# Gathering tokens feature-major for two experts at a time in a mixture-of-experts layer

## The chip, the cores and the metric

The kernel runs on one core of one Trainium2 chip. The metric is the device time of the whole kernel in microseconds; the median of the runs shown counts.

## What is computed

One layer on 256 tokens of width 2048, all in float32: an attention and state-space mixer, a layer norm, then sixteen experts of which each token uses two, and a per-layer embedding (PLE) that is gated by the same tokens. The change concerns the experts:

```python
combine = jnp.einsum('tk,tke->te', top_w, jax.nn.one_hot(top_idx, N_EXPERTS, dtype=f32))
out = jnp.zeros((b * s, d), f32)
for e in range(N_EXPERTS):
    hid = jax.nn.silu(xt @ w_gate[e]) * (xt @ w_up[e])
    out = out + combine[:, e:e + 1] * (hid @ w_down[e])
...
gate = jax.nn.sigmoid(jnp.einsum('bsd,de->bse', x, w_ple_gate))
return gate * jnp.einsum('bsk,kd->bsd', p_i, w_ple)
```

Here xt is the normed x, w_gate and w_up are 2048 x 1024 for each expert, and w_down is 1024 x 2048. The layer's last step is `layer_norm(DEEPNORM_ALPHA * h + moe + ple, ln2_g, ln2_b)`.

## The kernel before

The mixer, the first norm and the router take the first 447 us; the change does not touch them but for names of buffers. Then come the experts, one after the other, and a final norm from about 1480 us.

Each expert has places for CAP = 64 tokens. The one-hot matrix oh (128 tokens of a half x 64 places, doubled to 128 columns) says which token sits in which place. `gather(e)` multiplies it with h, the normed tokens before gain and bias: oh is stationary (64 columns), h moves in pieces of 512 columns (L679). That yields rows (places x features), which ACT copies to SBUF (L681) and which eight transposes (L689) turn to features x places; two DVE operations each (L693, L694) apply the norm's gain and bias and leave xg. Two transposes of oh (L697) give cm, the map that later returns the rows to the tokens, and two matmuls (L699) with the token weights cw give cwp, the weight of each place.

`gate_up(e)` takes 16 weight tiles of 1 MiB (128 x 2048 float32), eight of the gate and eight of the up matrix, and multiplies with xg stationary (L715). `hidden` makes the sigmoid (ACT L723), two products (DVE L724, L725, the second also by cwp), four transposes (L728) and ACT's copy hidT (L730). `down(e)` takes 8 tiles (L762, L784 in the last expert), and splits the result y into a high and a low part (ACT L752, DVE L753). `give_back` multiplies both with cm (L739), in the PSUM banks py, and DVE adds them to acc (L743). The banks py are also those that y comes from. Other PSUM banks are mt (gathers, transposes), gu (gate, up) and pl (PLE).

Weights run through a ring of sixteen tiles. SP issues each load once its slot is free (L76, L82, L87, L95 are its four buffers' lines), with at most eight loads under way. The order of loads is that of use: for each expert gate and up alternating, then down; ahead of experts 1, 4, 8 and 12 come four tiles of the PLE gate and one of ple, used behind the expert's down (`ple_gate`, L805 and L819). The order on each engine is made by a scheduler when the kernel is built; it pushes PLE matmuls and the next expert's gate matmuls between steps of the give-back.

After expert OV_AT = 6's hidden, `overflow` stands: all engines read a flag (how many tokens found no place) and branch past a loop over all experts (L826 reads it, L834 branches). With these inputs the loop is skipped, but SP, ACT and the others join there, and the buffers that the loop would use (tags y, xg, w2) are tied to it. The gather of expert e + 1 is written between hidden and down of expert e.

Of the kernel before, what the change touches and what calls it, by code (L numbers as in the profile page):

```python
# [27 lines left out]
OV_AT = 6  # L28
# [504 lines left out]
def back(ctx, tc, i, out, fr, dbg=lambda *a: None):  # L533
# [74 lines left out]
    r4 = mp.tile([128, 256], F32, name="r4", tag="cm", bufs=2)  # L608
# [58 lines left out]
    def gather(e):  # L667


        oh = mp.tile([128, NT, 2, CAP], F32, name="oh", tag="oh")  # L670
        for t in range(NT):
            nc.vector.tensor_scalar(oh[:, t], i1[:, None, :].to_broadcast([128, 2, CAP]), pos[:, t, e:e + 1], None,
                                    op0=OP.is_equal)
        rows = mp.tile([128, 1024], F32, name="rows", tag="y")
        for c in range(2):
# [6 lines left out]
        xg = mp.tile([128, 8, 2, CAP], F32, name="xg", tag="xg")  # L682
        b = [128, 4, 2, CAP]
        for c in range(2):
            ps = mt_psum(b)
            js = slice(4 * c, 4 * c + 4)
            for j in range(4):
                col0 = c * 512 + j // 2 * 256
                nc.tensor.transpose(ps[:, j].rearrange("p a b -> p (a b)"),  # L689
                                    rows[:, col0 + j % 2:col0 + 256:2], ident)  # L690
            gain, bias = (lnT[:, n, :].rearrange("p (d j) -> p j d", d=2)[:, js, :, None].to_broadcast(b)
                          for n in range(2))
            nc.vector.tensor_tensor(xg[:, js], ps, gain, op=OP.mult)  # L693
            nc.vector.tensor_tensor(xg[:, js], xg[:, js], bias, op=OP.add)  # L694
        ps = mt_psum([128, 512])
        for t in range(NT):
            nc.tensor.transpose(ps[:, t * 128:(t + 1) * 128], oh[:, t].rearrange("p a b -> p (a b)"), ident)  # L697
        for t in range(NT):
            nc.tensor.matmul(ps[:, 256:257], oh[:, t].rearrange("p a b -> p (a b)"), cw[:, t, e:e + 1],  # L699
                             start=t == 0, stop=t == 1)  # L700
        cm = mp.tile([128, 256], F32R, name="cm", tag="cm", bufs=2)
        cwp = mp.tile([128, 1], F32, name="cwp", tag="cwp", bufs=2)
        nc.scalar.activation(cm, ps[:, :256], AF.Copy)
        nc.vector.tensor_copy(cwp, ps[:, 256:257])
        return xg, cm, cwp

    def gate_up(e, xg):
        pgu = [psum.tile([128, 512], F32, name="pgu", tag="gu", bufs=2) for _ in range(2)]
        for k2 in range(8):
            for j in range(2):  # L710
                w = v2(ring.take(("gu"[j], e, k2)), FE)
                for r in range(2):
                    k = 2 * k2 + r
                    for fh, hs in H2:
                        mm = nc.tensor.matmul(pgu[j][hs], xg[:, k % 8, k // 8, :], w[:, r, fh * 512:(fh + 1) * 512],  # L715
                                         start=k == 0, stop=k == KB - 1)
            ring.fill()
        return pgu, mm

    def hidden(pgu, cwp):  # L720

        hid = mp.tile([128, 512], F32, name="hid", tag="w2", bufs=3)
# [10 lines left out]
    def give_back(cm, y, cols, n, pss):  # L733

        for t in range(NT):
            ps = pss(t)
            for j in range(2):
                for dh, hs in H2:
                    nc.tensor.matmul(ps[dh], cm[hs, t * 128:(t + 1) * 128], y[cols // 512][j][hs, cols % 512:cols % 512 + n],  # L739
                                     start=j == 0, stop=j == 1)  # L740
            for dh, hs in H2:
                a = acc[:, t, dh * 1024 + cols:dh * 1024 + cols + n]
                nc.vector.tensor_tensor(a, a, ps[dh], op=OP.add)  # L743

    def y_parts():
        y0 = mp.tile([128, 2, 512], F32R, name="y0", tag="y")
        y1 = [mp.tile([128, 512], F32R, name="y1", tag="w2", bufs=3) for _ in range(2)]
        return (y0[:, 0, :], y0[:, 1, :]), y1
# [6 lines left out]
    def down(e, hidT, cm):  # L755
# [13 lines left out]
        for c in range(2):  # L769
            def pss(t):  # L770
                p2 = psum.tile([128, 2, 512], F32, name="py", tag="y", bufs=1)
                return p2[:, 0, :], p2[:, 1, :]
            give_back(cm, y, c * 512, 512, pss)

    def down_last(e, hidT, cm):
        py = psum.tile([128, 2, 512], F32, name="py", tag="y", bufs=1)
        y = y_parts()
        for q in range(4):
# [11 lines left out]
            give_back(cm, y, q * 256, 256, pss)  # L790
# [18 lines left out]
    def ple_gate(c):  # L809
# [4 lines left out]
        for t in range(NT):  # L814
            sg = mp.tile([128, 512], F32, name="sg", tag="w2", bufs=3)
# [8 lines left out]
    def overflow():  # L824
# [9 lines left out]
        with tc.If(n_over > 0):  # L834
            with tc.For_i(0, NE, 1) as e:
                ovc = mp.tile([128, NT], F32, name="ovc")
                nc.sync.dma_start(ovc, scro[bass.ds(e, 1)].rearrange("o t p -> p (o t)"))
                oT = [mp.tile([128, 4, 256], F32, name="oT", tag=tag) for tag in ("y", "xg")]
                hd, *ow = [mp.tile([128, 512], F32, name="ow", tag="w2", bufs=3) for _ in range(3)]
                for fh in range(2):  # L840
# [8 lines left out]
                    for t in range(NT):  # L849
# [6 lines left out]
                        nc.scalar.activation(oT[fh][:, :, t * 128:(t + 1) * 128], ps, AF.Copy)  # L856
                for c in range(4):
                    cs = slice(c * 512, (c + 1) * 512)
                    pys = psum.tile([128, 2, 512], F32, name="py", tag="y", bufs=1)
                    for f in range(8):  # L860
                        w = wload(ow[f % 2], i["w_down"], e, f * 128, c * 512)
                        fh, j = divmod(f, 4)
                        for t in range(NT):
                            nc.tensor.matmul(pys[:, t, :], oT[fh][:, j, t * 128:(t + 1) * 128], w,
                                             start=f == 0, stop=f == 7)
# [7 lines left out]
    xg, cm, cwp = gather(0)  # L873

    lna = const.tile([16, 2, 128], F32, name="lna")
    with tc.issue_after(stats_done.ins):
        nc.vector.tensor_scalar(lna, fr.lnr[:, 0:2, :], ALPHA, None, op0=OP.mult)
# [23 lines left out]
    for e in range(NE):  # L901
        pgu, gated = gate_up(e, xg)
        hidT, cm_e = hidden(pgu, cwp), cm
# [5 lines left out]
        if e + 1 < NE:  # L909
            xg, cm, cwp = gather(e + 1)  # L910
            down(e, hidT, cm_e)
        else:
            down_last(e, hidT, cm_e)
        if e == 0:
# [14 lines left out]
            ovT = const.tile([NE, NT, 128], F32, name="ovT")  # L929
# [55 lines left out]
```

## Time and profile before

| | |
|---|---|
| Median of three runs | 1504.21 us (1503.3 to 1505.61) |
| The profiled execution | 1501.48 us, span 1499.8 us |
| Mean granted TensorE clock | 0.987 |
| TensorE busy | 1422.9 us, 95% of the span |
| DVE, ACT, POOL busy | 477.0, 291.9, 63.4 us |
| Moved | 499.96 MB, mean 333 GB/s |

The span runs from the first to the last instruction. TensorE's busy time is the sum of its matmuls; weight loads overlap it and are counted apart. The mean load rate hides that the rate differs from stretch to stretch.

### The profile page before, as it was taken

Reading aid. Unit: us, or ns where it says so; the run is one execution under the profiler, and the core shown is the slowest. Engines: PE = TensorE matmul, PEld = TensorE weight load, DVE = VectorE, ACT = ScalarE, POOL = GpSimd, SP = SyncE. Lnnn points to the kernel's source line nnn. Section 1 sums busy time; section 2 is a strip of 40 time slices with the busy share of each in tenths; the row PEclk is TensorE's granted clock in tenths of the full one; section 3 lists DMA queues with packets and bytes.
Section 4 is the critical chain, followed back from the end, with each engine's and each line's share of the span. In section 5 each row is a group of like instructions: output and inputs, shape, how many; then the busy total and the mean of one; then the engine's idle time right before and its main releaser. Section 6 shows DMA issues by size and latency. Waiting matters only on the chain. (4 is left out here: it accounts for less than half of the span.)

```text
span 1499.8 us, 15718 instructions
## 1 busy us (share of the span) xinstructions
PE 1422.9 (95%) x6467; PEld 703.5 (47%) x6467; DVE 477.0 (32%) x825; ACT 291.9 (19%) x445; POOL 63.4 (4%) x80
## 2 busy tenths in 40 slices
PE   7999999999989999999999989999999999999994
PEld 5878878777863433333233323323333332343332
DVE  4476774545651222112012211201221220202126
ACT  3465554444330010001010000000000000110001
POOL 3000011200000000000000000000000000000002
PEclk9999999999999999999999989999999999999997
DMA  8655555467858699999989999999999999899993
GB/s 275 186 171 167 190 192 194 155 224 291 291 188 341 264 420 392 417 420 410 352 332 420 419 419 377 409 420 369 420 419 420 420 409 412 365 420 420 420 386 118
DMA packets 116721, 499.96 MB, mean 333 GB/s; under 512 B 12692, under 2 KB 25436, under 8 KB 68260
## 3 DMA queue, kind: packets, MB, share of 16 engines
q1 hardware_dynamic: 115200, 495.42, 84.1%
q0 software_dynamic: 1408, 3.43, 0.8%
q8 instruction: 53, 0.87, 0.2%
q14 instruction: 24, 0.20, 0.0%
q10 hardware_dynamic: 36, 0.05, 0.0%
HBM read 496.70 MB, written 2.16 MB: 333 GB/s over the span
## 5 line engine op out<-in xcount | busy, mean ns | idle before, releaser
L715 PE MATMUL pgu<-ring,xg 128*64 128x512 f32 x2048 | 474.3, 598 | 2.0 <-DMA ring<-in_w_gate 1.4
L715 PEld LDWEIGHTS pgu<-ring,xg 128*64 128x64 f32 x2048 | 142.9, 137 | 293.5 <-issue 282.3
L762 PE MATMUL py<-ring,hidT 128*64 128x512 f32 x960 | 224.9, 595 | 0.0
L205 DVE TENSOR_TENSOR wl<-ring,wh 128x1024 fp32r<-128x1024 f32 x128 | 156.3, 1225 | 138.7 <-ACT wh L204 133.5
L204 ACT ACTIVATE wh<-ring 128x1024 fp32r<-128x1024 f32 x128 | 135.4, 1059 | 171.1 <-PE pj L211 151.5
L209 PE MATMUL pj<-wh,xh 128*128 128x512 f32 x384 | 154.1, 403 | 1.0 <-ACT xh L186 0.9
L210 PE MATMUL pj<-wl,xh 128*128 128x512 f32 x384 | 153.8, 401 | 0.0
L211 PE MATMUL pj<-wh,xl 128*128 128x512 f32 x384 | 153.1, 400 | 0.0
L724 DVE TENSOR_TENSOR hid<-hid,pgu 128x512 f32<-128x512 f32 x16 | 11.0, 687 | 409.7 <-ACT hid L723 409.7
L762 PEld LDWEIGHTS py<-ring,hidT 128*64 128x64 f32 x960 | 69.8, 137 | 131.7 <-issue 129.8
L805 PE MATMUL pl<-ring,hT 128*128 128x512 f32 x256 | 126.5, 617 | 0.0
L723 ACT ACTIVATE hid<-pgu 128x512 f32<-128x512 f32 x16 | 9.6, 597 | 509.8 <-PE pgu L715 509.8
L743 DVE TENSOR_TENSOR acc<-acc,py 128x512 f32<-128x512 f32 x120 | 77.1, 684 | 69.9 <-PE py L739 69.9
L753 DVE TENSOR_TENSOR y<-py,y 128x512 fp32r<-128x512 f32 (+1 forms) x34 | 22.4, 660 | 224.6 <-ACT y L752 224.6
L209 PEld LDWEIGHTS pj<-wh,xh 128*128 128x128 f32 x384 | 72.7, 189 | 18.1 <-ACT xh L186 2.1
L211 PEld LDWEIGHTS pj<-wh,xl 128*128 128x128 f32 x384 | 72.8, 189 | 16.6 <-DVE xl L187 0.2
L210 PEld LDWEIGHTS pj<-wl,xh 128*128 128x128 f32 x384 | 72.8, 190 | 16.1
L805 PEld LDWEIGHTS pl<-ring,hT 128*128 128x128 f32 x256 | 43.5, 189 | 73.2 <-issue 72.8
L679 PE MATMUL mt<-h,oh 128*64 128x512 f32 x256 | 63.8, 636 | 6.5 <-PEq L834 6.5
L752 ACT ACTIVATE y<-py 128x512 fp32r<-128x512 f32 (+1 forms) x34 | 19.4, 572 | 253.7 <-PE py L762 223.3
L739 PE MATMUL py<-y,cm 64*128 64x512 f32 x240 | 44.4, 447 | 18.5 <-DVE y L753 18.5
L209 PE MATMUL pj<-wh,moh 128*128 128x512 f32 (+1 forms) x160 | 56.7, 354 | 0.0
(261 smaller groups left out, 992.0 us busy)
## 6 DMA issues: line engine op xcount, KB each, us to landing
ring<-in_w_gate SPq DMA_DIRECT2D x128, 1024.0 KB, 16.0
ring<-in_w_up SPq DMA_DIRECT2D x128, 1024.0 KB, 16.1
ring<-in_w_down SPq DMA_DIRECT2D x120, 1024.0 KB, 16.6
ring<-in_w_in SPq DMA_DIRECT2D x48, 1024.0 KB, 5.1
ring<-in_w_out SPq DMA_DIRECT2D x16, 1024.0 KB, 6.0
ring<-in_w_ple_gate SPq DMA_DIRECT2D x32, 512.0 KB, 11.2
ring<-in_w_down SPq DMA_DIRECT2D x16, 512.0 KB, 8.8
xq<-in_x SPq DMA_DIRECT2D x8, 256.0 KB, 9.6
```

The lines of the kernel that those rows point to most:

```text
L204: nc.scalar.activation(h, v, AF.Copy)
L205: nc.vector.tensor_tensor(l, v, h.bitcast(F32), op=OP.subtract)
L209: nc.tensor.matmul(ps, ah, bh, start=first, stop=False)
L210: nc.tensor.matmul(ps, ah, bl, start=False, stop=False)
L211: nc.tensor.matmul(ps, al, bh, start=False, stop=last)
L679: nc.tensor.matmul(ps[hs], oh[:, t, 0, :], h[:, t, dh * 1024 + c * 512:dh * 1024 + (c + 1) * 512], start=t == 0, stop=t == 1)
L715: mm = nc.tensor.matmul(pgu[j][hs], xg[:, k % 8, k // 8, :], w[:, r, fh * 512:(fh + 1) * 512], start=k == 0, stop=k == KB - 1)
L739: nc.tensor.matmul(ps[dh], cm[hs, t * 128:(t + 1) * 128], y[cols // 512][j][hs, cols % 512:cols % 512 + n], start=j == 0, stop=j == 1)
L743: nc.vector.tensor_tensor(a, a, ps[dh], op=OP.add)
L753: nc.vector.tensor_tensor(yl, ps, yh.bitcast(F32), op=OP.subtract)
L762: nc.tensor.matmul(py[hs, c, :], hidT[:, j, fh * 64:(fh + 1) * 64], w[:, dh * 1024 + c * 512:dh * 1024 + (c + 1) * 512], start=fb == 0, st ...
L805: nc.tensor.matmul(pg[t], hT[:, k, t * 128:(t + 1) * 128], w[:, r, :], start=k == 0, stop=k == KB - 1)
```

## The change

`gather` now serves two experts: it is called for 0 and 1 before the loop, and at each odd e for e + 1 and e + 2. h is stationary, 128 columns with a stride of two (one feature block), and the one-hot columns of both experts move (128 columns); the product is feature-major at once, for 16 blocks and two token halves 32 matmuls (L681 of the new kernel). They are evicted in groups of four blocks, two groups by DVE (product and sum with gain and bias), two by ACT (four operations with scale and bias each). rows and its transposes are gone, xg is twice as large and lives over two experts. The map cm is made per expert by `places`, behind gate_up. cwp is gone: the weight is applied per token when the returned rows are added to acc, with the same number of DVE operations. The first half of each give-back (t = 0) uses two mt banks in place of py. Buffers shrink (w2 from 3 to 2, cm from 2 to 1) to pay for xg, and since the overflow loop uses xg's buffer, OV_AT moves from 6 to 7.

```diff
-OV_AT = 6
+OV_AT = 7
...
-            ps = mt_psum([128, 512])
-            for t in range(NT):
-                for dh, hs in H2:
-                    nc.tensor.matmul(ps[hs], oh[:, t, 0, :], h[:, t, dh * 1024 + c * 512:dh * 1024 + (c + 1) * 512],
-                                     start=t == 0, stop=t == 1)
-            nc.scalar.activation(rows[:, c * 512:(c + 1) * 512], ps, AF.Copy)
...
-                nc.tensor.transpose(ps[:, j].rearrange("p a b -> p (a b)"),
-                                    rows[:, col0 + j % 2:col0 + 256:2], ident)
...
+        oh = mp.tile([128, NT, 2, 2, CAP], F32, name="oh", tag="oh")
+        for t in range(NT):
+            for j in range(2):
+                nc.vector.tensor_scalar(oh[:, t, j], i1[:, None, :].to_broadcast([128, 2, CAP]),
+                                        pos[:, t, e + j:e + j + 1], None, op0=OP.is_equal)
+        xg = mp.tile([128, KB, 2, CAP], F32, name="xg", tag="xg")
+        for k4 in range(4):
+            ps = mt_psum([128, 4, 2, CAP])
+            ks = range(4 * k4, 4 * k4 + 4)
+            for k in ks:
+                cols = slice(k // 2 * 256 + k % 2, (k // 2 + 1) * 256, 2)
+                for t in range(NT):
+                    nc.tensor.matmul(ps[:, k % 4], h[:, t, cols], oh[:, t, :, 0, :], start=t == 0, stop=t == 1)
+            if k4 % 2:
+                for k in ks:
+                    nc.scalar.activation(xg[:, k], ps[:, k % 4], AF.Identity, bias=lnT[:, 1, k:k + 1],
+                                         scale=lnT[:, 0, k:k + 1])
+            else:
...
+                nc.vector.tensor_tensor(v, p, gain, op=OP.mult)
+                nc.vector.tensor_tensor(v, v, bias, op=OP.add)
+        return xg, oh
+
+    def places(e, oh):
+
+        ps = mt_psum([128, 256])
+        for t in range(NT):
+            nc.tensor.transpose(ps[:, t * 128:(t + 1) * 128], oh[:, t, e % 2].rearrange("p a b -> p (a b)"), ident)
+        cm = mp.tile([128, 256], F32R, name="cm", tag="cm")
+        nc.scalar.activation(cm, ps, AF.Copy)
+        return cm
...
-        nc.vector.scalar_tensor_tensor(hid, hid, cwp, pgu[1], op0=OP.mult, op1=OP.mult)
+        nc.vector.tensor_tensor(hid, hid, pgu[1], op=OP.mult)
...
-                nc.vector.tensor_tensor(a, a, ps[dh], op=OP.add)
+                nc.vector.scalar_tensor_tensor(a, ps[dh], cw[:, t, e:e + 1], a, op0=OP.mult, op1=OP.add)
...
             def pss(t):
+                if t == 0:
+                    return [mt_psum([128, 512]) for _ in range(2)]
                 p2 = psum.tile([128, 2, 512], F32, name="py", tag="y", bufs=1)
...
-        hidT, cm_e = hidden(pgu, cwp), cm
+        cm = places(e, oh)
+        hidT = hidden(pgu)
...
-            xg, cm, cwp = gather(e + 1)
-            down(e, hidT, cm_e)
+            if e % 2:
+                xg, oh = gather(e + 1)
+            down(e, hidT, cm)
```

TensorE's order between gate/up and down of expert 2, before (every expert reads like this; hid are the hidden transposes):

```order
L728 MATMUL mt<-ident,hid 128x128 x4
L679 MATMUL mt<-h,oh 64x512 x8
L689 MATMUL mt<-ident,rows 128x128 x4
L762 MATMUL py<-ring_4344,hidT 64x512
L689 MATMUL mt<-ident,rows 128x128 x4
L697 MATMUL mt<-ident,oh 128x128 x2
L699 MATMUL mt<-cw,oh 128x1 x2
L762 MATMUL py<-ring_4344,hidT 64x512 x3
```

The same place of the changed kernel (L711, L723, L681, L735 and L758 are the new lines of gate/up, hidden transposes, gather, give-back and down; L698 are the transposes for the map):

```order
L711 MATMUL pgu<-ring_4317,xg 64x512 x4
L698 MATMUL mt<-ident,oh 128x128 x2
L711 MATMUL pgu<-ring_4333,xg 64x512 x4
L723 MATMUL mt<-ident,hid 128x128 x4
L758 MATMUL py<-ring_4345,hidT 64x512 x4
```

and in expert 3:

```order
L711 MATMUL pgu<-ring_4490,xg 64x512 x4
L711 MATMUL pgu<-ring_4496,xg 64x512 x4
L723 MATMUL mt<-ident,hid 128x128 x4
L681 MATMUL mt<-oh,h 128x128 x32
L758 MATMUL py<-ring_4545,hidT 64x512 x4
```

In even experts nothing stands between the hidden transposes and down any more; the gather of odd ones is one block of 32.

TensorE's order at the give-back of a plain expert, before:

```order
L715 MATMUL pgu<-ring_4392,xg 64x512 x3
L739 MATMUL py<-y_4532,cm 128x512 x4
L715 MATMUL pgu<-ring_4392,xg 64x512
L715 MATMUL pgu<-ring_4394,xg 64x512 x3
L739 MATMUL py<-y_4532,cm 128x512 x4
```

and now (y_4498 is the first half's y, y_4499 and y_4500 the second half's two parts):

```order
L758 MATMUL py<-ring_4383,hidT 64x512 x4
L735 MATMUL mt<-y_4498,cm 128x512 x2
L711 MATMUL pgu<-ring_4393,xg 64x512
L735 MATMUL mt<-y_4498,cm 128x512 x2
L711 MATMUL pgu<-ring_4393,xg 64x512 x2
L735 MATMUL py<-y_4498,cm 128x512 x4
```

The first half goes to mt and stands directly behind down; three gate matmuls stood ahead of it before.

SP's order ahead of the branch, before (gate and up of expert 7):

```order
L82 DMA ring2_5400<-in_w_up 128x2048 [waits DMAHW2_49,PE_49]
L82 DMA ring2_5410<-in_w_gate 128x2048 [waits DMAHW3_49,PE_49]
L82 DMA ring1_5412<-in_w_up 128x2048 [waits DMAHW4_49,PE_49]
L82 DMA ring0_5422<-in_w_gate 128x2048 [waits DMAHW5_49,PE_49]
L82 DMA ring0_5424<-in_w_up 128x2048 [waits DMAHW6_49,PE_49]
L826 TENSOR_LOAD flag_4046 [waits DVE_49]
```

and now, where the last PLE gate half of expert 8's stage, ple and three tiles of expert 8 stand ahead:

```order
L87 DMA ring0_5580<-in_w_ple_gate 128x2x512 [waits DMAHW6_49]
L76 DMA ring4_5591<-in_w_ple 128x2x512 [waits DMAHW7_49,PE_49]
L82 DMA ring4_5593<-in_w_gate 128x2048 [waits DMAHW0_49,PE_49]
L82 DMA ring4_5603<-in_w_up 128x2048 [waits DMAHW1_49,PE_49]
L82 DMA ring4_5605<-in_w_gate 128x2048 [waits DMAHW2_49,PE_49]
L824 TENSOR_LOAD flag_4026 [waits DVE_49]
```

The branch has moved behind twenty-eight more loads, the rest of gate and up of expert 7, all of its down, the PLE stage's and three tiles of expert 8.

## Rows read from the trace of the kernel before

**Rows 1.** Stretches: us, busy TensorE, its loads, DVE, ACT, POOL; clock, DMA share, GB/s.

```profile
725.00:775.00 50.00, 49.15 (x193) 16.30 (x194) 4.66 (x9) 2.77 (x5) 0.00 (x0) 1.00 0.82 311
...
775.00:900.00 125.00, 112.61 (x506) 39.10 (x504) 23.57 (x40) 9.02 (x16) 2.54 (x2) 0.96 1.01 419
...
905.00:910.00 5.00, 3.56 (x18) 1.03 (x16) 1.38 (x2) 1.19 (x2) 0.00 (x0) 1.00 0.39 116
...
910.00:975.00 65.00, 62.76 (x274) 21.56 (x276) 15.49 (x26) 3.96 (x7) 0.00 (x0) 1.00 1.02 413
...
1025.00:1050.00 25.00, 25.00 (x104) 8.46 (x99) 3.92 (x8) 2.27 (x5) 0.00 (x0) 1.00 0.85 341
...
875.00:890.00 15.00, 7.89 (x25) 3.04 (x26) 0.73 (x2) 1.79 (x3) 0.00 (x0) 0.66 1.01 417
```

**Rows 2.** Chain of waits around expert 8: start us, us, what.

```profile
954.80 11.83 DMA ring<-in_w_gate
...
966.67 1.07 PE pgu L715 x2
...
980.15 1.91 PE pl L805 x4
...
1057.42 1.87 PE pgu L715 x8
```

**Rows 3.** Timeline from 1404 us: start us, us, engine, line, instructions, idle before.

```profile
1404.13 3.65 PE L679 MATMUL mt<-h,oh 128*64 128x512 f32 x16
...
1409.97 0.38 PE L697 MATMUL mt<-ident,oh 128*128 128x128 f32 x2
...
1410.19 0.50 PE L699 MATMUL mt<-cw,oh 128*128 128x1 f32 x4
...
1410.63 13.52 PE L762 MATMUL py<-ring,hidT 128*64 128x512 f32 x61
```

**Rows 4.** Timeline from 447 us: the first gather and that in expert 0.

```profile
447.69 3.65 PE L679 MATMUL mt<-h,oh 128*64 128x512 f32 x16
...
454.17 27.69 PE L715 MATMUL pgu<-ring,xg 128*64 128x512 f32 x128 [0.58 <-DVE xg L694]
...
484.54 5.34 PE L679 MATMUL mt<-h,oh 128*64 128x512 f32 x14
```

**Rows 5.** Timeline from 425 us: transposes of h, and evictions by ACT.

```profile
434.97 1.48 ACT L595 ACTIVATE hT<-bk,lnT 128x256 f32<-128x256 f32 x3
...
435.15 0.57 PEld L591 LDWEIGHTS py<-ident,h 128*128 128x128 f32 x4
...
435.63 0.33 PEld L591 LDWEIGHTS bk<-ident,h 128*128 128x128 f32 x2
```

**Rows 6.** Timeline from 1456 us: the last expert, without a gather behind it.

```profile
1459.52 2.81 PE L784 MATMUL py<-ring,hidT 128*64 128x256 f32 x24 [0.69 <-ACT hidT L730]
```

**Rows 7.** Groups by form from 660 us on: one-hot builds.

```profile
L672 DVE TENSOR_SCALAR oh<-i,pos 128x128 f32<-128x128 f32 x22 | 6.1, 278 | 0.0
```

**Rows 8.** Timeline from 1424 us: a give-back.

```profile
1424.67 0.60 ACT L752 ACTIVATE y<-py 128x512 fp32r<-128x512 f32 x1 [13.55 <-PE py L762]
...
1426.65 0.69 DVE L753 TENSOR_TENSOR y<-py,y 128x512 fp32r<-128x512 f32 x1 [0.66 <-ACT y L752]
...
1427.40 0.73 PE L739 MATMUL py<-y,cm 64*128 64x512 f32 x4 [1.97 <-DVE y L753]
```

**Rows 9.** Timeline from 570 us: a give-back behind PLE matmuls.

```profile
575.73 0.73 PE L739 MATMUL py<-y,cm 64*128 64x512 f32 x4
```

**Rows 10.** Timeline from 870 us: the branch.

```profile
882.76 6.26 PE L679 MATMUL mt<-h,oh 128*64 128x512 f32 x16 [6.52 <-PEq L834]
...
888.10 0.33 SPq L82 DMA_DIRECT2D ring<-in_w_up  x1
...
908.16 0.34 SPq L82 DMA_DIRECT2D ring<-in_w_gate  x1
...
908.46 0.60 ACT L752 ACTIVATE y<-py 128x512 fp32r<-128x512 f32 x1 [1.95 <-SPq L834]
```

More of the change, by code (lines that the diff above doesn't have):

```diff
@@ L695, in gather @@
-        ps = mt_psum([128, 512])
-        for t in range(NT):
[L697 to L702, printed above, removed]
@@ L703, in gather @@
-        nc.scalar.activation(cm, ps[:, :256], AF.Copy)
-        nc.vector.tensor_copy(cwp, ps[:, 256:257])
-        return xg, cm, cwp
+            for j in range(2):
[14 more added lines that the diff above has]
+            else:
+                b = [128, 4, 2 * CAP]
+                v, p = (a.rearrange("p k e c -> p k (e c)") for a in (xg[:, ks.start:ks.stop], ps))
+                gain, bias = (lnT[:, n, ks.start:ks.stop, None].to_broadcast(b) for n in range(2))
+                nc.vector.tensor_tensor(v, p, gain, op=OP.mult)
+                nc.vector.tensor_tensor(v, v, bias, op=OP.add)
@@ L718, in gate_up, with hidden @@
         return pgu, mm
-    def hidden(pgu, cwp):
-        hid = mp.tile([128, 512], F32, name="hid", tag="w2", bufs=3)
+    def hidden(pgu):
+        hid = mp.tile([128, 512], F32, name="hid", tag="w2", bufs=2)
         nc.scalar.activation(hid, pgu[0], AF.Sigmoid)
         nc.vector.tensor_tensor(hid, hid, pgu[0], op=OP.mult)
-        nc.vector.scalar_tensor_tensor(hid, hid, cwp, pgu[1], op0=OP.mult, op1=OP.mult)
+        nc.vector.tensor_tensor(hid, hid, pgu[1], op=OP.mult)
         ps = mt_psum([128, 4, 128])
@@ L742, in give_back @@
                 a = acc[:, t, dh * 1024 + cols:dh * 1024 + cols + n]
-                nc.vector.tensor_tensor(a, a, ps[dh], op=OP.add)
+                nc.vector.scalar_tensor_tensor(a, ps[dh], cw[:, t, e:e + 1], a, op0=OP.mult, op1=OP.add)
     def y_parts():
         y0 = mp.tile([128, 2, 512], F32R, name="y0", tag="y")
-        y1 = [mp.tile([128, 512], F32R, name="y1", tag="w2", bufs=3) for _ in range(2)]
+        y1 = [mp.tile([128, 512], F32R, name="y1", tag="w2", bufs=2) for _ in range(2)]
         return (y0[:, 0, :], y0[:, 1, :]), y1
@@ L814, in ple_gate @@
         for t in range(NT):
-            sg = mp.tile([128, 512], F32, name="sg", tag="w2", bufs=3)
+            sg = mp.tile([128, 512], F32, name="sg", tag="w2", bufs=2)
             nc.scalar.activation(sg, pg[t], AF.Sigmoid)
@@ L837, in overflow @@
                 nc.sync.dma_start(ovc, scro[bass.ds(e, 1)].rearrange("o t p -> p (o t)"))
-                oT = [mp.tile([128, 4, 256], F32, name="oT", tag=tag) for tag in ("y", "xg")]
-                hd, *ow = [mp.tile([128, 512], F32, name="ow", tag="w2", bufs=3) for _ in range(3)]
+                oT = mp.tile([128, 2, 4, 256], F32, name="oT", tag="xg")
+                hd = mp.tile([128, 512], F32, name="hd", tag="w2", bufs=2)
+                ow2 = mp.tile([128, 2, 512], F32, name="ow", tag="y")
+                ow = ow2[:, 0, :], ow2[:, 1, :]
                 for fh in range(2):
@@ L872, in back @@
         ple_sums(0, range(PLE_FIRST))
-    xg, cm, cwp = gather(0)
-    lna = const.tile([16, 2, 128], F32, name="lna")
+    xg, oh = gather(0)
+    lna = fr.lnr[:, 0:2, :]
     with tc.issue_after(stats_done.ins):
-        nc.vector.tensor_scalar(lna, fr.lnr[:, 0:2, :], ALPHA, None, op0=OP.mult)
+        nc.vector.tensor_scalar(lna, lna, ALPHA, None, op0=OP.mult)
     def row_bank(ps, rows, c):
```

34 lines of the change are left out of this document (9 added, 25 removed).

## The prediction

> **What bounds the kernel now.** I read the page's busy shares first, then the stretches table, the chain of waits, and last the timelines around one gather, one give-back and the branch. TensorE is busy almost throughout, so the first thought is that every instruction taken from it is time gained. The stretches table says where that holds [rows 1]. From 725 to 775 us and from 1025 to 1050 us the loads move only 311 and 341 GB/s at a busy TensorE: the ring of weight tiles is full and the loads wait for TensorE to free a slot. From 775 to 900 and from 910 to 975 us they move 419 and 413 GB/s without a pause. That is the most the queue ever moves, so a tile of 1 MiB (1.049 MB) takes 2.5 us. An expert needs 24 tiles, 60 us, and TensorE's period for an expert without a PLE stage is shorter (54.7 us, from the end of one expert's hidden transposes at 1404.13 to the end of the next one's, 0.69 ahead of 1459.52) [rows 3, 6]. The ring drains by some 5 us in each plain expert and refills where a PLE stage gives TensorE about 34 us of work for 11 us of loads. It runs dry once: at 966.67 TensorE stands before a tile of expert 8, and the chain of waits turns to a DMA piece of 11.83 us [rows 2]. So there are three stretches: experts 0 to 4, where TensorE sets the time; experts 5 to 8, where the loads do; experts 9 to 15, TensorE again.
>
> **The gather, per instruction.** One old gather runs from 1404.13 to 1410.63, 6.50 us, with two L762 instructions inside (13.52/61 x 2 = 0.44): 6.06 us net per expert [rows 3]. The first took 6.48 from 447.69 to the gate matmuls at 454.17, and the one in expert 0 ran 2.2 us over, 5.34 us for 14 of its 16 matmul instructions against 3.65 for 16 [rows 3, 4]. The new gather is 32 matmuls, 64 instructions with 128 columns stationary and 128 moving, for two experts. The trace has no such matmul. The nearest row is L591, h stationary with the same stride of two and 128 columns moving: four loads from 435.15 to 435.63, 0.120 us each [rows 5]. From below, four L699 instructions with 128 stationary columns and one moving took 0.44 us, 0.11 each [rows 3]; from above, that load and a stream of 128 columns (a quarter of the 0.43 that a pair of 512-column L762 instructions takes) one after the other, 0.21. I take 0.120 since L591 has the same operand and stride: 64 x 0.120 + 0.2 for the switch = 7.9 us per pair of experts, against 12.1. Evicting: ACT's three 256-column copies with scale and bias took 1.48 us [rows 5], so four 128-column ones take under 2 us, about the 1.92 us that TensorE works on a group of four blocks; DVE has the other groups. I cost the evictions at nothing; if ACT were 0.5 us late twice per gather, it is 1 us per pair.
>
> **What is added per expert.** The two transposes for the map back (before 1409.97 to 1410.19, 0.22, and a switch each way) now stand inside the gate/up matmuls: 0.5 us, 16 times [rows 3]. In even experts the hidden transposes are followed at once by the down matmuls, which wait for ACT's copy. Expert 15 of before shows that wait, 0.69 us, and a switch: 0.75 us [rows 6]. It stands in experts 2 to 14; in expert 0 the residual's work covers it. In experts 1 and 9 four one-hot builds of 0.278 us stand on DVE ahead of the hidden product [rows 7] that TensorE waits for: 0.6 us each. The token's weight moves from the hidden product to the accumulation, the same DVE forms in swapped places: nothing. ACT and POOL lose a little that nobody waits for.
>
> **The give-back.** Before, its first matmuls need py's banks, released only when both halves are split: ACT from 1424.67, DVE's last split from 1426.65, TensorE idle 1.97 us to 1427.40 [rows 8]. Now the first half's two banks come from the spare pool and need the first split alone, 1.35 us earlier, but only one gate instruction pair stands between instead of three. Net I take 0.6 us less wait in plain experts. Where PLE matmuls stood ahead of it before (experts 1, 3, 11), the row has no wait at all [rows 9]; now one PLE matmul, not four, stands ahead: 1.8 us more.
>
> **Stretch by stretch.** Experts 0 to 4. Old: 6.5 + 5 x 6.06 + 2.2 = 39.0. New: 3 x 7.9 + 5 x 0.5 + 2 x 0.75 + 0.6 + (2 x 1.8 - 2 x 0.6) = 30.7. Gain 8.3.
>
> Experts 9 to 15. Old: 6 x 6.06 = 36.4. New: 3 x 7.9 + 7 x 0.5 + 3 x 0.75 + 0.6 + (1.8 - 5 x 0.6) = 28.9. Gain 7.5.
>
> Experts 5 to 8 go by the loads. TensorE's own savings there (about 7 us) are not kept, since the tile it waits for lands no sooner than the 8.3 us that its slot was freed earlier. But the branch moves. At the branch SP must see all eight outstanding loads land: its last issue before is at 888.10, the next at 908.16, and from 905 to 910 us the loads fall to 116 GB/s, 3.6 us lost [rows 1, 10]. The split of y behind the branch waits on ACT for the same thing [rows 10]. Before, this stood behind gate/up of expert 6 with slack in the ring. Now it stands behind expert 7's, and SP's order ahead of the branch holds down 7, the four PLE gate tiles, ple and three tiles of expert 8. So y of expert 7 waits until the third of these has landed: 966.67 + 2 x 2.5 = 971.7 by the old stream [rows 2], 3.6 earlier since its hole is yet to come, so 968.1 - 8.3. TensorE's own way from the last gate/up tile of expert 7 to y (1.7 + 2.5 for the hidden product, 6.5 for the branch, 7.9, 13.8 for down) is 32 us, and the 15.5 tiles that must land take 38.8, so it idles some 6 us there. Then the hole, 3.6, and the next tile at 974.2; twelve more tiles at 2.5 put the last gate/up tile of expert 8 at 1004.2, its matmuls end at 1005.9 and its hidden transposes start at 1008.4 (all less 8.3). What then remains before expert 9's gate/up is TensorE's: 1.3 + 13.8 down + 60 PLE instructions at 1.91/4 = 0.478, 28.7 [rows 2], + 2.7 give-back + 3.6 for ple + 1.0 of waits = 51.1, so 1059.5 - 8.3. Before, the same point is 1057.42 less 1.3 for gate matmuls already done and plus 0.66 for a give-back still to do: 1056.7 [rows 2]. Loss 2.8, because PLE's 28.7 us no longer lies beside the loads of gate/up 8 but behind them.
>
> **The sum.** -8.3 + 2.8 - 7.5 = -13.0. The profiled execution took 1501.5 us and becomes 1488.5; the median of the runs is 2.7 us above it, so 1491.
>
> **The rivals.**
> *The loads do not bind in experts 5 to 8.* If the ring stays ahead, because stretch 1 fills it earlier and the wait for y is short, all of TensorE's savings count: 8.3 + 7 + 7.5 = 22.8, 1481. Against it stands 419 GB/s without a pause for 125 us [rows 1]. 0.15.
> *The ring stays dry behind expert 8.* PLE now ends with a ring that started late; were it not full again by expert 9, the last stretch would be set by loads too and its 7.5 us not kept: 1499. For it speaks that the 5 us per plain expert are drawn down more quickly when TensorE's period shrinks by 1.1 us an expert; against it that 28.7 us of PLE bring in about eleven tiles. 0.18.
> *The new matmul does not hide its load.* At 0.21 us instead of 0.12, a gather costs 5.8 us more; six of the eight lie in stretches that TensorE sets: +34.6, 1525, slower than before. It turns to slower from 0.155 us per instruction (13.0/384 above 0.120). Against it L591 at 0.120 with transposes [rows 5]; for it, that a true matmul of this shape does not occur. 0.10. The Trainium skill, "TensorE: Matmul & The Clock Gate", section "LDWEIGHTS (loading the stationary operand)", has the load's time go by the stationary operand's columns, 107 ns for 128 of them, which speaks against making h with its 128 columns stationary in place of 64 one-hot columns. By that figure alone a gather would be an estimated 6.8 us and the time 1485; the 0.11 us of L699 agrees with it, and whether stream and load overlap is what it leaves open.
> *The clock falls at the new waits.* Behind 6.5 us of idling at the old branch the granted clock was 0.66 from 875 to 890 us, part of it at the lower level of 1.2 GHz, and L679 took 6.26 us instead of 3.65 [rows 1, 3, 10]. One such stretch at each of the seven experts of the last part is 7 x 2.6 = 18, 1509. Against it: the new waits there are shorter than the old 1.97 us. 0.05. The Trainium skill has the same on that page, section "HAM oscillation — how this bites in real kernels": bursts of matmuls with waits for data between them each pay the lower clock. By it the long wait before y of expert 7 is followed by slow matmuls; here that hides behind the loads and adds nothing to the sum.
>
> **How the numbers follow.** Forecast 0.52, the rivals 0.15, 0.18, 0.10 and 0.05. The range holds the forecast, 1481 and 1499 with the small terms' bounds (1 us per pair of evictions, 2 us of median spread): 1479 to 1503; 0.15 lies above. About 0.2%, 3 us, is what a measurement can tell from no change. Faster: forecast, the first rival and most of the second, 0.77; same, the rest of the second and what lies between, 0.10; slower, 0.13.
>
> **What would show it.** Right: L681 at about 7.7 us for 64; L723 to L758 with a 0.7 us wait in even experts; a wait of some 6 us for y behind the branch, the load rate dropping once for about 4 us there, expert 9's gate/up starting some 6 us earlier than before, and the last give-back some 13 us earlier. Wrong: 64 instructions in over 10 us; DMA waits of TensorE behind expert 9; TensorE's lower clock level outside the branch; expert 8 starting without a wait for tiles.

## The result, and the profile after

The changed kernel takes 1477.26 us (median of 4 runs, 1476.23 to 1478.99) against 1504.91 for the kernel before on the same chip: ratio 0.9818, 95% interval 0.9801 to 0.9835, 27.6 us faster. The forecast was 1491 with a range of 1479 to 1503; the sign was right, the gain about twice the forecast and the time below the range.

The two profiled executions are 22.9 us apart, not 27.6: their spans are 1499.8 and 1476.9 us. The one before was 3.4 us below its median (1501.5 against 1504.9), the one after 1.7 us above (1479.0). The comparison by stages below is made between these two traces.

| Start of the hidden transposes of expert | before, us | after, us | difference | forecast |
|---|---|---|---|---|
| 5 | 820.88 | 809.46 | -11.4 | -8.3 |
| 9 | 1085.83 | 1076.96 | -8.9 | -5.5 |
| 15 | 1458.18 | 1434.51 | -23.7 | -13.0 |
| last instruction's end | 1499.8 | 1476.9 | -22.9 | -13.0 |

So the forecast gave the middle stretch, experts 5 to 8, almost exactly (2.5 us lost against 2.8), and was short by 3 us ahead of it and by 7 us behind it.

The first view is the timeline of the changed kernel around expert 10's down and give-back, an even expert without a gather. Columns are start, duration, engine, line, instructions, and in brackets the idle time ahead with what ended it.

```profile
1132.95 0.66 PE L723 MATMUL mt<-ident,hid 128*128 128x128 f32 x4 [0.79 <-DVE hid L720]
1134.29 13.95 PE L758 MATMUL py<-ring,hidT 128*64 128x512 f32 x64 [0.69 <-ACT hidT L725]
1148.94 0.50 PE L735 MATMUL mt<-y,cm 64*128 64x512 f32 x2 [0.70 <-ACT y L748]
1149.37 1.07 PE L711 MATMUL pgu<-ring,xg 128*64 128x512 f32 x2
```

The wait for hidT is the 0.69 us of [rows 6], as forecast. The give-back's first matmuls wait 0.70 us, and what releases them is ACT's copy alone; in [rows 8] it was 1.97 us and DVE's split.

The same view of expert 11, which has a gather behind its hidden transposes and PLE matmuls at its give-back:

```profile
1181.98 0.66 PE L723 MATMUL mt<-ident,hid 128*128 128x128 f32 x4 [0.79 <-DVE hid L720]
...
1182.48 7.70 PE L681 MATMUL mt<-oh,h 128*128 128x128 f32 x64
...
1190.11 13.95 PE L758 MATMUL py<-ring,hidT 128*64 128x512 f32 x64
...
1190.22 1.50 ACT L684 ACTIVATE xg<-mt,lnT 128x128 f32<-128x128 f32 x4 [2.26 <-PE mt L681]
...
1203.99 1.12 PE L803 MATMUL pl<-ring,hT 128*128 128x512 f32 x2
...
1205.05 0.50 PE L735 MATMUL mt<-y,cm 64*128 64x512 f32 x2
...
1205.48 1.13 PE L803 MATMUL pl<-ring,hT 128*128 128x512 f32 x2
```

The gather runs from 1182.48 to 1190.11, 7.63 us for 64 instructions, 0.119 us each, the 0.120 of [rows 5]. ACT's four evictions take 1.50 us and nobody waits for them. At the give-back one PLE matmul covers ACT's copy, and L735 has no wait; the forecast had charged 1.8 us here.

Then the branch. The rows are the timeline from 905 us on, of TensorE (PE), ACT and SP's queue.

```profile
927.88 9.38 PE L681 MATMUL mt<-oh,h 128*128 128x128 f32 x64 [6.37 <-PEq L832]
...
944.67 0.33 SPq L82 DMA_DIRECT2D ring<-in_w_gate  x1
953.95 1.04 PE L711 MATMUL pgu<-ring,xg 128*64 128x512 f32 x2 [2.80 <-SPq L832]
...
959.02 0.60 ACT L748 ACTIVATE y<-py 128x512 fp32r<-128x512 f32 x1 [20.21 <-SPq L832]
...
959.30 0.34 SPq L82 DMA_DIRECT2D ring<-in_w_up  x1
...
959.67 0.80 PE L735 MATMUL mt<-y,cm 64*128 64x512 f32 x2 [4.67 <-ACT y L748]
...
996.17 1.94 PE L711 MATMUL pgu<-ring,xg 128*64 128x512 f32 x8
...
999.00 0.60 PE L723 MATMUL mt<-ident,hid 128*128 128x128 f32 x4
```

y of expert 7 is split at 959.02 (forecast 968.1 - 8.3 = 959.8), SP issues nothing between 944.67 and 959.30, TensorE waits 2.80 + 4.67 = 7.5 us (forecast 6), the last gate/up tile of expert 8 is used at 996.17 (forecast 995.9) and its hidden transposes start at 999.00 (forecast 1000.1). The matmuls behind the branch are slow, 9.38 us for 64 instructions instead of 7.70, at a granted clock of 0.81 in that stretch; as forecast, that lies on time that the loads own.

Last, the stretches (us, busy TensorE, its loads, DVE, ACT, POOL; clock, DMA share, GB/s):

```profile
450.00:525.00 75.00, 75.00 (x366) 33.71 (x364) 14.78 (x22) 5.16 (x12) 0.00 (x0) 0.98 0.76 290
525.00:775.00 250.00, 244.86 (x1069) 92.89 (x1068) 43.42 (x71) 18.83 (x40) 3.12 (x3) 1.00 1.00 411
775.00:925.00 150.00, 137.52 (x644) 49.66 (x640) 28.57 (x48) 11.23 (x23) 2.54 (x2) 1.00 1.01 420
...
950.00:975.00 25.00, 17.50 (x68) 5.22 (x66) 6.83 (x10) 1.19 (x2) 0.00 (x0) 0.80 0.83 340
975.00:1440.00 465.00, 450.68 (x2020) 170.96 (x2016) 72.09 (x115) 37.37 (x75) 5.08 (x4) 1.00 1.01 416
```

Two of these stretches in the kernel before:

```profile
525.00:775.00 250.00, 245.36 (x1012) 85.97 (x1010) 46.12 (x78) 16.90 (x30) 2.52 (x2) 1.00 0.97 390
...
975.00:1440.00 465.00, 448.53 (x1926) 156.03 (x1924) 81.14 (x137) 34.70 (x61) 5.09 (x4) 1.00 1.00 410
```

The loads now run at 416 GB/s from 975 to 1440 us. The kernel before moved 410 there as a mean, with dips such as the 341 of [rows 1], so they were close to their limit in the last third already; the larger difference lies ahead, 411 against 390 from 525 to 775 us. The long pauses left are ahead of 525 us and at the branch: (420 - 340)/420 of 25 us is 4.8 us there. The chain of waits of the changed kernel shows it too:

```profile
972.62 20.41 DMA ring<-in_w_gate
...
1048.55 27.64 PE pgu L711 x128
...
1444.42 8.98 DMA ring<-in_w_down
```

In [rows 2] the DMA piece was 11.83 us long; now there is one of 20.41 us, and a second one at the very end, before the last expert's last tiles. Expert 9's gate/up begins at 1048.55.

### The profile page after: what moved, and what is told of

It reads as the page before. It is cut to its first block, busy times and chain, and to the rows that moved or that the text cites. A ratio compares the mean times of both kernels' runs of the same rounds, so it can differ in the third digit from the quotient of the medians.

```text
span 1476.9 us, 15862 instructions
## 1 busy us (share of the span) xinstructions
PE 1396.7 (95%) x6531; PEld 725.8 (49%) x6531; DVE 459.5 (31%) x777; ACT 297.1 (20%) x477; POOL 62.9 (4%) x80
## 5 line engine op out<-in xcount | busy, mean ns | idle before, releaser
L711 PE MATMUL pgu<-ring,xg 128*64 128x512 f32 x2048 | 475.3, 599 | 9.8 <-DMA ring<-in_w_gate 3.5
L711 PEld LDWEIGHTS pgu<-ring,xg 128*64 128x64 f32 x2048 | 141.3, 137 | 299.2 <-issue 267.3
L758 PE MATMUL py<-ring,hidT 128*64 128x512 f32 x960 | 210.6, 594 | 4.1 <-ACT hidT L725 4.1
L758 PEld LDWEIGHTS py<-ring,hidT 128*64 128x64 f32 x960 | 67.1, 137 | 137.5 <-issue 126.9
L681 PE MATMUL mt<-oh,h 128*128 128x128 f32 x512 | 63.4, 286 | 6.4 <-PEq L832 6.4
L681 PEld LDWEIGHTS mt<-oh,h 128*128 128x128 f32 x512 | 62.7, 201 | 7.1 <-issue 7.0
L210 PE MATMUL pj<-wl,moh 128*128 128x512 f32 (+1 forms) x160 | 56.4, 353 | 0.0
## 6 DMA issues: line engine op xcount, KB each, us to landing
ring<-in_w_up SPq DMA_DIRECT2D x128, 1024.0 KB, 17.4
```

Of the source, the lines that this page charges most:

```text
L210: nc.tensor.matmul(ps, ah, bl, start=False, stop=False)
L681: nc.tensor.matmul(ps[:, k % 4], h[:, t, cols], oh[:, t, :, 0, :], start=t == 0, stop=t == 1)
L711: mm = nc.tensor.matmul(pgu[j][hs], xg[:, k, e % 2, :], w[:, r, fh * 512:(fh + 1) * 512], start=k == 0, stop=k == KB - 1)
L758: nc.tensor.matmul(py[hs, c, :], hidT[:, j, fh * 64:(fh + 1) * 64], w[:, dh * 1024 + c * 512:dh * 1024 + (c + 1) * 512], start=fb == 0, st ...
```

## The experiments

All were timed against the kernel before on the same chip. The medians of the changed kernel and of before are those above; before's medians in the three later comparisons were 1504.5, 1503.4 and 1503.0. A difference to the changed kernel is thus one between comparisons that lie up to 1.9 us apart; where it is small, the ratios and their intervals (0.9801 to 0.9835 for the changed kernel) decide.

### The parts of the give-back

**The spare banks alone.** The kernel before, with this in `down`:

```diff
             def pss(t):
+                if t == 0:
+                    return [mt_psum([128, 512]) for _ in range(2)]
                 p2 = psum.tile([128, 2, 512], F32, name="py", tag="y", bufs=1)
```

> The kernel before, with one part of the change alone: the first token half of each give-back goes to two spare PSUM banks instead of py. Theory A (the give-back's first matmuls need only ACT's high part of y, so their wait falls from 1.97 to about 0.7 us): about 1.3 us at each of the eleven plain experts, less the two or three in experts 5 to 8 where the loads set the pace: 10 to 12 us faster, 1493 to 1495, and a wait of about 0.7 us ahead of the give-back in the trace. Theory B, the term of the prediction (0.6 us less wait, since the first split by ACT and DVE must both be done): 4 to 6 us faster, wait about 1.4 us.

Measured: 1497.3 us, ratio 0.9957 (0.9940 to 0.9973), 7.2 us faster. Its timeline at expert 13's give-back:

```profile
1364.85 0.60 ACT L752 ACTIVATE y<-py 128x512 fp32r<-128x512 f32 x1 [13.55 <-PE py L762]
...
1365.50 0.50 PE L739 MATMUL mt<-y,cm 64*128 64x512 f32 x2 [0.75 <-ACT y L752]
```

The wait is theory A's: 0.75 us, released by ACT's copy. The gain is between the two theories: from expert 13's hidden transposes to 14's it takes only 0.38 us less (1343.71 to 1398.03, 54.32 us, against 1348.84 to 1403.54, 54.70, in the kernel before), since the down matmuls now take 14.95 us instead of 13.94: the trace has the last two down instructions one behind the other, with no gate matmul beside them.

**The spare banks taken out of the changed kernel.** The reverse edit.

> The changed kernel, with the give-back's first half back in py. Theory A: the wait ahead of a plain give-back returns from 0.7 to about 2.0 us, in seven late and three early experts: 10 to 13 us slower than the changed kernel, 1487 to 1490. Theory B: 0.6 us each, 5 us slower, 1482. If the loads had so much say in the late experts that the wait hides behind them: 2 to 3 us slower, from the early experts alone.

Measured: 1475.9 us, ratio 0.9812 (0.9796 to 0.9829): not slower at all. Theories A and B fall here, and so does the third expectation, 2 to 3 us slower. From expert 13's hidden transposes to expert 15's it takes 104.92 us, against 104.89 with the banks. Its give-back:

```profile
1350.15 1.88 PE L711 MATMUL pgu<-ring,xg 128*64 128x512 f32 x6
...
1350.37 0.60 ACT L748 ACTIVATE y<-py 128x512 fp32r<-128x512 f32 x1 [12.90 <-PE py L758]
...
1353.16 0.73 PE L735 MATMUL py<-y,cm 64*128 64x512 f32 x4 [1.13 <-DVE y L749]
```

It waits for DVE's second split again, yet only 1.13 us and not 1.97. ACT's copy starts 0.22 us behind the first of the gate matmuls that fill the wait. In the kernel before it starts at 1424.67, 1.1 us behind the first of them at 1423.56. So something else in the change has made y come earlier against TensorE's queue. What stood just ahead there, and is gone, is the old gather with the down matmul in its midst; the next experiment tests that.

**Down in one piece.** The kernel before, with down kept behind the gather:

```diff
-            xg, cm, cwp = gather(e + 1)
-            down(e, hidT, cm_e)
+            xg, cm, cwp, mm = gather(e + 1)
+            with tc.issue_after(mm.ins):
+                down(e, hidT, cm_e)
```

(mm is the gather's last matmul, L699.)

> The kernel before, with the one down matmul that stood between the gather's transposes put behind the gather, and nothing else. Theory P (that lone matmul, two instructions on half the columns, shifts the pairing of all the later half-column matmuls, so the last one of down ends 0.85 us later against the gate matmuls beside it, and y is late by as much): the wait ahead of a plain give-back falls from 1.97 to about 1.1 us, the gather waits about 0.3 us for ACT's copy of its second rows; 0.5 us per expert, 4 to 5 us faster, 1499 to 1500. Rival (the wait is all ACT's and DVE's splits): wait still 1.97, the gather's new wait comes on top, 3 to 6 us slower.

Measured: 1490.8 us, ratio 0.9919 (0.9893 to 0.9945), 12.6 us faster. Theory P holds in its mechanism, and its size was too small. First the kernel before, at expert 13's down, then this kernel at the same place:

```profile
1353.68 1.07 PE L762 MATMUL py<-ring,hidT 128*64 128x512 f32 x2
...
1354.69 0.74 PE L689 MATMUL mt<-ident,rows 128*128 128x128 f32 x4
...
1368.85 0.59 PE L715 MATMUL pgu<-ring,xg 128*64 128x512 f32 x1
...
1369.28 0.59 PE L762 MATMUL py<-ring,hidT 128*64 128x512 f32 x1
...
1369.28 1.45 PE L715 MATMUL pgu<-ring,xg 128*64 128x512 f32 x5
...
1369.96 0.60 ACT L752 ACTIVATE y<-py 128x512 fp32r<-128x512 f32 x1 [13.55 <-PE py L762]
...
1372.77 0.73 PE L739 MATMUL py<-y,cm 64*128 64x512 f32 x4 [2.03 <-DVE y L753]
```

```profile
1345.68 13.95 PE L762 MATMUL py<-ring,hidT 128*64 128x512 f32 x64
...
1359.46 1.88 PE L715 MATMUL pgu<-ring,xg 128*64 128x512 f32 x6
...
1359.74 0.60 ACT L752 ACTIVATE y<-py 128x512 fp32r<-128x512 f32 x1 [13.57 <-PE py L762]
...
1362.54 0.73 PE L739 MATMUL py<-y,cm 64*128 64x512 f32 x4 [1.20 <-DVE y L753]
```

Before, the last L762 instruction starts at 1369.28, behind the first L715 at 1368.85 and beside the next: two instructions on 64 of the 128 columns run side by side, and the one matmul drawn out of the row (1353.68, its two instructions on the same 64 columns) has shifted all later pairs by one. y is late by about 0.8 us for that. With down in one piece, all 64 end together, the wait falls to 1.20 us, and an expert takes 54.05 us instead of 54.70. The rival, a wait that is all splits, is out. Expected was 0.5 us in plain experts; it is 0.65, and in those with a PLE stage too: 10.9 us between the traces. Of these some 1.6 lie between experts 9 and 10, where the trace of before has a stretch at the lower clock (granted 0.87 from 1104 to 1112 us); whether the edit has to do with that is not shown.

**Both.** The two edits together on the kernel before.

> The kernel before, with both: down in one piece behind the gather, and the give-back's first half in spare banks. Theory P: the wait falls to 0.7 us and no lone down matmul remains, about 1 us per plain expert: 8 to 10 us faster, 1494 to 1496, about as far as the spare banks alone, which had kept the lone matmul. If the two parts add (7 of the spare banks, 5 of the whole down): 12 us faster, 1492.

Measured: 1488.1 us, ratio 0.9901 (0.9878 to 0.9924), 15.3 us faster. By the medians the parts do not add up to 7 + 12.6: the banks bring 2 to 3 us more once down is whole, with intervals that overlap. In plain experts they do add: from expert 13's hidden transposes to 14's the kernel before takes 54.70 us, 54.32 with the banks, 54.05 with down in one piece and 53.66 with both. What is missing lies outside them: in the traces, experts 5 to 8 gained less than the two parts together, and the stretch at the lower clock in the trace of before stands in the gain of either part. The total is more than either expectation had, since the whole down had brought more.

### Who sets the time

**Late gathers left out.** The changed kernel with

```diff
-            if e % 2:
+            if e % 2 and e < 9:
                 xg, oh = gather(e + 1)
```

so that experts 10 to 15 compute with the tokens of experts 8 and 9.

> The changed kernel, the gathers at experts 9, 11 and 13 left out (experts 10 to 15 use the tokens of 8 and 9): TensorE has 3 x 7.6 = 23 us less to do in the last part. Theory L (the loads run without a pause from 775 us on and the ring is empty by the last tiles, so they set the end): at most 2 us faster, about 1475, with waits for weight tiles in experts 11 to 15 that add up to some 20 us. Theory T (TensorE sets the time from expert 9 on): 23 us faster, 1454.

Measured: 1475.1 us, ratio 0.9809 (0.9793 to 0.9825), 2.2 us below the changed kernel and not to be told from it by the intervals: theory L, and far from theory T's 23. In its timeline TensorE stands before nine tiles of expert 15 in a row, of which these are the first two:

```profile
1404.77 1.94 PE L711 MATMUL pgu<-ring,xg 128*64 128x512 f32 x8 [0.52 <-DMA ring<-in_w_up]
1407.24 1.94 PE L711 MATMUL pgu<-ring,xg 128*64 128x512 f32 x8 [0.54 <-DMA ring<-in_w_gate]
```

At expert 14 it is 17 us ahead of the changed kernel (1368.25 against 1385.46), and at the end 4.6 us in the traces, 2.2 in the medians: the rest went into waits for tiles. Of the 4.6, 3.3 were there at expert 9 already, ahead of the first gather that is left out.

**Early gathers left out.** The same for the gathers at experts 1 and 3 (`e % 2 and e > 3`); experts 2 to 5 compute with the tokens of 0 and 1.

> The changed kernel, the gathers at experts 1 and 3 left out (experts 2 to 5 use the tokens of 0 and 1): TensorE has 15 us less to do before 775 us. Theory L: there the loads wait for slots, so all later loads move forward; 10 to 15 us faster, 1462 to 1467, less what the loads lack of pauses in that part. Theory T: 15 us faster less what experts 5 to 8 take back, 1462 to 1470. If the loads already had no pause to give there: no change.

Measured: 1471.5 us, ratio 0.9781 (0.9764 to 0.9797), 5.8 us faster than the changed kernel. Theory L had 10 to 15 and theory T 7 to 15, and both are wrong on the size; the third expectation, no change, is wrong too: at expert 5 it is 12.2 us ahead (797.29 against 809.46), at expert 9 6.0. Even in the early experts the loads had few pauses left to give: from 525 to 775 us they move 418 GB/s against the changed kernel's 411, and by their landings in the trace TensorE uses the last down tiles of expert 3 as they land.

**No branch.** The changed kernel without the call of `overflow`.

> The changed kernel without the branch for tokens that found no place (with these inputs its loop is never run). Theory L (the loads set the time from 775 us on): what is saved is their gap at the branch, 4 to 5 us: 1472 to 1473, the loads at 419 or 420 GB/s in every stretch behind 775 us. Theory T (TensorE's waits at the branch set it: 6.4 us to pass it, some 10 us for y): 15 us faster, 1462.

Measured: 1472.1 us, ratio 0.9791 (0.9766 to 0.9815), 5.2 us below the changed kernel in the medians and 5.6 in the traces, about 4 by the ratios, whose intervals overlap: theory L, and far from theory T's 15. The trace shows how. At expert 9 this kernel is 17.4 us ahead of the changed one (1059.61 against 1076.96); at expert 11 it is 8.1 us ahead, at the end 5.6. Between lies this row of its timeline, two like it behind it, and nine more in expert 11's gate/up. The tiles come 2.49 us apart there, and TensorE needs 27.64/16 = 1.73 for one:

```profile
1126.35 1.94 PE L758 MATMUL py<-ring,hidT 128*64 128x512 f32 x8 [0.55 <-DMA ring<-in_w_down]
```

**The branch elsewhere.** OV_AT = 5 in place of 7.

> The changed kernel with the branch behind expert 5's gate/up in place of expert 7's, so that expert 8's PLE stage no longer waits behind it. Theory L: the loads' gap moves along with the branch, the time stays within 3 us of the changed kernel's 1477. Theory T: the loss of expert 9 (15 us against the kernel before) goes, 8 to 12 us faster, 1465 to 1469.

Measured: 1476.0 us, ratio 0.9831 (0.9805 to 0.9856): not to be told from the changed kernel, theory L. At expert 9 it is 15.7 us ahead, as theory T had it, and all but 3.8 us of the traces' difference is given back by the end.

**PLE stages at other experts.** `PLE_AT = (2, 5, 8, 11)` in the changed kernel:

> The changed kernel with the PLE stages behind experts 2, 5, 8 and 11 in place of 1, 4, 8 and 12; TensorE's work and the bytes are the same. Theory L (the loads set the time; what they lose is lost before 525 us, where the ring is full and they run at 250 to 270 GB/s, and at the branch): the first stage comes later, so the ring is emptied earlier, and the last one comes earlier, so the ring isn't empty at the end: 5 to 15 us faster than the changed kernel, 1462 to 1472. Theory T (TensorE's work sets it): no change, within 3 us of 1477.

Measured: 1479.5 us, ratio 0.9853 (0.9831 to 0.9875): no gain. The gain that theory L gave here did not come, and the number is theory T's, no change. The trace still shows why it is not TensorE's work that sets it. The loads' pause ahead of 525 us shrinks little (270 and 296 GB/s in the two slices of the page there, against 245 and 267), and new pauses arise at other places (361 and 386 GB/s where the stage behind expert 11 has filled the ring). Stages behind 3, 6, 9 and 12:

> The changed kernel with the PLE stages behind experts 3, 6, 9 and 12. Theory L: the first stage later still, but the last one as late as now, so less is gained than with 2, 5, 8, 11: 3 to 10 us faster than the changed kernel. Theory T: no change.

Measured: 1474.2 us, ratio 0.9813 (0.9794 to 0.9832), 3 us below the changed kernel in the medians, 1 by the ratios, and not to be told from it by the intervals: theory T's number again, at the edge of theory L's. And stages behind 2, 5, 8 and 11 with the branch behind 3:

> As the kernel with stages behind 2, 5, 8, 11, and the branch behind expert 3 in place of 7, where the ring has just been filled behind a stage. Theory L: within 3 us of the same kernel with the branch at 7, since the loads' gap of 4 to 5 us only moves. Theory T (waits at the branch): up to 6 us apart.

Measured: 1476.7 us, ratio 0.9825 (0.9808 to 0.9843), 2.8 us from the kernel with the same stages and the branch at 7, which both theories allow. So the kernels with moved PLE stages do not tell the theories apart by their times; those without late gathers, without the branch and with the branch elsewhere do. In all the traces under this heading TensorE takes the last down tiles of expert 15 as they land, within 1.5 us. No kernel here that keeps all gathers beats the changed one by more than the intervals.

The kernel before with the stages behind 2, 5, 8 and 11:

> The kernel before with its PLE stages behind 2, 5, 8 and 11. If the loads bind in the kernel before only around expert 8 (one wait of 1.4 us of TensorE for a tile): within 4 us of before, 1500 to 1505. If they bind as in the changed kernel: 5 to 15 us faster.

Measured: 1508.8 us, ratio 1.0037 (1.0023 to 1.0051), 5.7 us slower, outside both. TensorE has few waits in it; the gate/up matmuls between expert 0's and expert 5's hidden transposes were busy 4.6 us longer (151.6 against 147.0). Why is open. It does not bear on the change.

## Why the prediction was wrong

**What bounds the kernel: right for the kernel before, and no longer for the last stretch after.** Three stretches, the middle one set by loads, was right: 2.5 us lost against 2.8, and the points in it within about 1 us but for two: TensorE's wait, 7.5 against 6, and expert 9's gate/up, 1048.55 against 1059.5 - 8.3 = 1051.2, since the last 30 PLE instructions ran in a block at 13.07/30 = 0.436 us and not the 0.478 of [rows 2]. In the last stretch the kernel before still had tiles in hand: the first half of the last one landed at 1468.94 us and was used from 1476.51 on. In the changed kernel these are 1451.96 and 1452.78: the loads, which the forecast held off experts 9 to 15, now end together with TensorE.

**The gather: right.** 0.119 us per instruction against 0.120, and 7.63 us a pair against 7.9. The load of 128 columns does hide behind the stream of 128; that rival is out. The evictions cost nothing. The old gather was put at 6.06 us net by counting the two down instructions in its midst at 0.44. Start to start they took 1.0 us, so TensorE's time for the gather itself was 5.50; the difference comes back in the rest of down, which is shorter by one pair. For experts 9 to 15 the gathers and maps fell from 32.97 to 25.16 us and down by 0.94, together 8.8; the forecast had 36.4 to 27.2, 9.2.

**Small terms.** The hidT wait: 2.06 us in three experts against 2.25. Maps: 0.35 us each against 0.5. The one-hot builds ahead of the hidden product: nothing, against 0.6 twice; the waits for the hidden product did not grow (0.79 us each).

**The give-back: the step that failed.** The forecast was 0.6 us less in plain experts and 1.8 us more where PLE stands. Measured between expert 9's and 15's hidden transposes, the idle time ahead of the give-back's matmuls fell from 9.89 to 3.49 us, -6.4 against the forecast's -1.2 (five plain experts at 1.97 and then 0.70 us, and none where PLE stands); between the first gather and expert 5's hidden transposes from 4.05 to 1.39, -2.7 against +2.4. Together 10.3 us, the miss of 9.9 between the traces. The lines of the sum, experts 9 to 15:

| | before, us | after, us | difference | forecast |
|---|---|---|---|---|
| gathers, maps, down's pairs | 117.56 | 108.81 | -8.8 | -9.2 |
| wait for hidT | 0 | 2.06 | +2.1 | +2.25 |
| wait ahead of the hidden transposes | 5.08 | 4.75 | -0.3 | +0.6 |
| wait ahead of the give-back | 9.89 | 3.49 | -6.4 | -1.2 |
| gate/up matmuls | 176.98 | 175.96 | -1.0 | 0 |
| all else | 62.84 | 62.48 | -0.4 | 0 |
| sum | 372.35 | 357.55 | -14.8 | -7.5 |

(Each is TensorE's time from the start of one instruction to the start of the next, with the idle time ahead of it counted apart. The gate/up matmuls lost one stretch at the lower clock that the trace of before had from 1104 to 1112 us.)

It failed in two ways. First, it took the first half's split as one piece, ACT and DVE; the order shown ahead of the prediction has two L735 alone, then a gate matmul, then two more, and the first two need only ACT's part. Second, it did not see that the old wait of 1.97 us had 0.8 us from the lone down matmul, which the change removed with the gather. The experiments tell these apart. Down in one piece by itself brings 12.6 us, the spare banks by themselves 7.2, both 15.3; and in the changed kernel the banks bring nothing. Without them the scheduler puts six gate instructions ahead of the give-back and, in even experts, the next map into hidT's wait: over experts 13 and 14 TensorE waits 0.8 us more ahead of the give-back, 0.2 less for hidT, and the rest is made up in the order of its instructions. So of the 27.6 us about 13 are what down in one piece brings by itself, and most of the remaining 15 come from the gather. From expert 9 to 15 the traces have 372.35 us before, 366.75 with down in one piece and 357.80 in the changed kernel without banks; the last step is 8.95 us, and gathers and maps fell by 9.4 in it. The gather's share is the difference between whole kernels (1490.8 of the kernel with down in one piece, and 1475.9 of the changed one without banks), not an experiment of its own.

**The basis.** 4.7 us of the miss lie between traces and medians. The trace of after lost 1.7 us to a stretch at the lower clock in expert 0 (granted 0.89 from 485 to 500 us; 112 PLE instructions take 54.5 us, 52.9 in the kernel without late gathers, which is the same up to there); the profiled execution of before lay 1.8 us below the fastest of its other runs, which the forecast had set against the median as 2.7.

**The rivals.** None of the rivals and no chance stood below 1479; the forecast had no case in which the give-back saves more. The time came out near the rival in which the loads do not bind (1481), but for another reason: they bind more than forecast. Its mechanism is refuted by the kernels without late gathers and without the branch. The rival of the ring that stays dry was wrong for the changed kernel, but barely: expert 15's last down tile is waited for, and 23 us of TensorE's work taken from there give 2.2. No waits at the lower clock appeared outside the branch in experts 9 to 15 (granted clock 1.00 from 975 to 1440 us). At the branch, behind the wait of 6.37 us, the granted clock was 0.81 from 927.88 to 937.26 us, part of it at the lower level of 1.2 GHz, and 64 instructions took 9.38 us; they cost nothing since y came later still. The Trainium skill, "TensorE: Matmul & The Clock Gate", section "HAM oscillation — how this bites in real kernels", has bursts of matmuls start at the lower clock behind long waits for data; the trace agrees at this place, though the wait here was one at the branch.

## What to carry to other kernels

Look at what a scheduler has put into the middle of a row of half-width matmuls: a single one drawn out shifted the pairs of all its successors, and the result at the row's end came about 0.8 us late, behind each of fifteen gathers. When a wait is costed, ask of each waiting instruction which of its operands it needs, and read the order for it; the first one often needs less than the group. And where two resources are nearly in balance, a saving on one is worth only what the other has left: here 23 us of TensorE's time were worth about 2, and 17 us won at one place were 5 or 6 at the end.

## What the hardware showed unexpectedly

Two matmul instructions on 64 columns each run side by side if they use different halves of the 128: 64 of them took 13.95 us, 0.218 each, while one matmul standing alone, two instructions on the same half, took 1.0 us from its start to the next instruction's (1353.68 to 1354.69). Beside each other the last of one row and the first of the next also pair, so a row with an odd start ends beside its successor's first instructions.

The new matmul, 128 columns stationary with a stride of two and 128 moving, ran at 0.119 us per instruction, at the pace that the transposes of the same operand had in the kernel before; loading the stationary operand added nothing to it that shows.
